# A decoder layer on one core: convolutions, low parts and norms given to other steps and engines

## The chip, the core and the metric

The kernel runs on one core of a Trainium2 chip. The metric is the device time of one execution in microseconds. TensorE (PE) multiplies, VectorE (DVE), ScalarE (ACT) and GpSimd (POOL) work elementwise, SyncE (SP) issues the transfers. Every engine takes its own instructions in order; they wait for each other by semaphores.

## The reference

One step of a hybrid decoder layer for 1024 prompt tokens and 32 sample tokens (8 sequences of 4), width 1024: adaLN, an mLSTM and a sliding-window attention branch, then a feed-forward part with a convolution over tokens. The change touches the last part alone (weights and gates left out where they don't matter):

```python
h2 = ln0(x) * (1 + scale2) + shift2
u = h2 @ w_up + b_up                       # 2 * 2816 columns
u = conv_w[2]*u[t] + conv_w[1]*u[t-1] + conv_w[0]*u[t-2] + conv_b   # causal, per column
act = gelu(u[:, :2816]) * u[:, 2816:]
x = LN2(alpha * x + gate2 * (act @ w_down + b_down))
```

The outputs also hold the last two tokens of `u` of every sequence.

## The kernel before

**Products.** All products are made of three fp32r products: each operand is a high part (`hi`, a cast by ACT) and a low part (`lo`, the rest, one subtraction). The weights come through a stream of blocks: `Stream.load` issues the transfer of a raw block into a slot of SBUF, `Stream.prep` has ACT cast the high part (L429) and `low_by` subtract the low part (L433), and frees the raw slot. `low_by` is DVE until the down groups, POOL from there on (L2120).

**Columns.** The 1056 tokens stand in the free dimension, 384 + 384 + 288 (`TT`). The 44 blocks of 128 columns of `u` are numbered 0 to 43; column `j` of the gelu half belongs to column `22 + j`. Columns 0 to 3 and 22 to 25 are made early by ordinary products; columns 20, 42, 21 and 43 by the four *direct blocks* (`up_direct`, 1607 to 1658 us), whose banks ACT empties (L1754); the other 32 by 16 *pairs* `j` = 4 to 19 (`fast`, 1270 to 1606 us), each 14 products long for both columns `j` and `22 + j`, over a ring of eight PSUM banks. When a pair's column is finished, `ff_finisher` decides: `u` of column `j` goes to DRAM as it is, column `22 + j` gets its convolution (`post`) beside the following pair and then goes to DRAM as `y`.

**Convolution.** `conv` is a generator: ACT makes the first tap and small copies (L1764 to L1769), DVE the two long taps (L1771, L1773) and two small ones for the sample tokens (L1775, L1776), with a `yield` after each part.

**Side work.** PE's instructions are the program's backbone. Each `pulse` of a product advances a program clock by its length times `rate[0]` (0.5 in the pairs, 0.9 in the direct blocks, 0.8 in the down groups); as the clock goes on, generators in `sides` are advanced by one step, and things put off by `later(us, ...)` are emitted. So the yields decide where an instruction stands in its engine's order.

**Feed.** `feed` (L1837) runs beside the direct blocks and the down groups. Item by item, in the order 4 to 11, 0, 20, 12, 13, 1, 21, 14, 15, 16, 2, 3, 17, 18, 19, it loads the two columns from DRAM, convolves column `j` (both columns for 0 to 3, 20 and 21), applies gelu (ACT, L1867), multiplies (DVE, L1872), casts the high part (ACT, L1881) and subtracts the low one (`alo`, DVE, L1886). Item n's convolution and item n-1's gelu and product share steps.

**Down groups.** `act @ w_down` runs in five groups of 5, 5, 4, 4 and 4 items (`KG`). Groups 0 to 2 go over eight output blocks `j`, each with three products (one for each part of `TT`) into the three banks `L`. Group 0 (1658 to 1717 us) writes `facc` by ACT (L1990); groups 1 to 3 add to it by DVE (L1992). Group 3 goes by tokens and is scaled by the gate; 72 transposes (`pre`) turn `facc` to rows. In group 4 (1889 to 1942 us) rows are made by products of 512 columns, two for each of nine row tiles.

**Tail.** For each row tile `i`, `add` sums on DVE, `stats` takes mean and variance (`mv`, DVE), 1/std on POOL (`rstd`, two operations) and, for `i` < 8, the factor `nbias` (POOL) and the normalisation on ACT; `gains(i - 1)` multiplies by the gain (L2179) on POOL for tiles 0 to 6 and on DVE for tile 7, and adds the bias on POOL (L2180). Tile 8, of 32 rows, goes on DVE alone (L2184, L2185).

Of the kernel before, what the change touches and what calls it, by code (L numbers as in the profile page):

```python
# [105 lines left out]
def hybrid_step(ctx: ExitStack, tc: tile.TileContext, I, O):  # L106
# [282 lines left out]
    class Stream:  # L389
        def __init__(self, specs):  # L390
            self.specs = specs
            self.raws, self.parts, self.loaded, self.limit = {}, {}, 0, len(specs)
            self.low_by = V
# [19 lines left out]
        def prep(self, i, later_lo=False):  # L413
# [24 lines left out]
            low()  # L438
# [1398 lines left out]
    def feed():  # L1837
# [3 lines left out]
        def load(n):  # L1841
            if n < len(js) and n not in got:
                ds = [uD[js[n]], yD[22 + js[n]] if 22 + js[n] in yD else uD[22 + js[n]]]
                got[n] = [slot(name="ld") for _ in ds]
                for t, d in zip(got[n], ds):
                    S.dma_start(t, d)
# [5 lines left out]
        for n in range(len(js) + 1):  # L1852
            cur = None
            if n < len(js):
                while len(free_slots) < ROOM:
                    yield
                load(n + 1)
                j, (u, y2) = js[n], got.pop(n)
                if 22 + j not in yD:
                    u2, y2 = y2, slot(name="y")  # L1860
                    yield from conv(22 + j, u2, y2)
                    drop(u2)
                    yield
                cur = slot(name="y"), y2
                taps = conv(j, u, cur[0])
            if prev:
                A.activation(prev[0], prev[0], AF.Gelu_apprx_tanh)  # L1867
            if cur:
                next(taps)
# [4 lines left out]
            if cur:  # L1874
                next(taps)
                if len(free_slots) > ROOM:
                    load(n + 2)
# [4 lines left out]
            if cur:  # L1882
                next(taps)
# [5 lines left out]
            if cur:  # L1889
                next(taps, None)  # L1890
                drop(u)
            yield
# [147 lines left out]

    def ff_finisher(j):
        return lambda blk_, z: sides.append(post(22 + j, z)) if blk_ else to_dram(uD, j, z)
# [77 lines left out]
    win.low_by = G  # L2120
# [21 lines left out]
    BY_POOL = (0, 1, 2, 3, 4, 5, 6)  # L2142
# [23 lines left out]
    def stats(i):  # L2166
        n = rows_of(i)
        mv = ln_stats(xs_[i], n)
        if i < 8:
            factor[i] = norm_factor(mv, n)  # L2170
            norm_act(xs_[i], factor[i], n)
        else:
            factor[i] = (mv, rstd(mv[:n, 1:2], n))

    def gains(i):
        n = rows_of(i)
        x = xs_[i][:n, :D]
        if i < 8:
            (G if i in BY_POOL else V).tensor_tensor(x, x, ln2g[:n, :D], op=OP.mult)  # L2179
            G.tensor_tensor(x, x, ln2b[:n, :D], op=OP.add)  # L2180
            dst = dap(O["yp"], i * 128 * D, [[D, 128], [1, D]])
        else:
# [3 lines left out]
            dst = dap(O["ys"], 0, [[D, 32], [1, D]])  # L2186
# [50 lines left out]
```

## Time and profile before

| | |
|---|---|
| median of 3 runs | 1960.11 us (1959.96 to 1962.17) |
| the profiled execution | 1961.27 us, span 1959.5 us |
| PE busy | 1904.9 us, 97% of the span |
| DVE busy | 1075.2 us, 55% |
| ACT busy | 804.9 us, 41% |
| POOL busy | 478.5 us, 24% |

The time is the span and what lies around it, 1.8 us here. The profile tells of one execution. Its times are from the span's start; the stages above are given in them.

### The profile page before, as it was taken

The numbers are of one execution on the slowest core, as the hardware profiler recorded it, in microseconds if no ns is written. First come the engines' busy times: TensorE is split into PE (matmuls) and PEld (weight loads), VectorE is DVE, ScalarE is ACT, GpSimd is POOL, SyncE is SP. The second block draws the span as 40 slices with busy tenths as digits, with TensorE's granted clock in tenths as the row PEclk, the third lists the DMA queues.
The fourth block names the chain that finished last, engine by engine and source line by source line (L and its number), as shares of the span: only waits on it lengthen the run. The fifth ranks groups of instructions, "written<-read, shape, count | busy, mean of one in ns | idle before, by whom it ended". The sixth has DMA issues, their size and how long they took to land. (4 is left out here: it accounts for less than half of the span.)

```text
span 1959.5 us, 32996 instructions
## 1 busy us (share of the span) xinstructions
PE 1904.9 (97%) x12981; PEld 1815.8 (93%) x12981; DVE 1075.2 (55%) x2293; ACT 804.9 (41%) x1796; POOL 478.5 (24%) x595
## 2 busy tenths in 40 slices
PE   6999999999999999999999999999999999999996
PEld 4899999999989989899999999999999999999884
DVE  5454444444545445332354445756666666778767
ACT  4534343343555455430322255332332336754521
POOL 2004233232022131200000243133434320222228
PEclk9999999999999999999999999999999999999998
DMA  9151524234211312298523242423232256444342
GB/s 292 48 141 19 148 25 131 59 97 79 92 67 33 113 45 86 74 338 278 165 96 101 72 127 69 143 87 123 88 120 100 96 169 214 156 132 146 128 154 89
DMA packets 233766, 232.24 MB, mean 119 GB/s; under 512 B 11665, under 2 KB 206913, under 8 KB 233577
## 3 DMA queue, kind: packets, MB, share of 16 engines
q1 hardware_dynamic: 232829, 229.51, 38.2%
q8 instruction: 102, 1.67, 0.4%
q10 hardware_dynamic: 780, 0.61, 0.1%
q14 instruction: 55, 0.45, 0.1%
HBM read 172.18 MB, written 59.93 MB: 118 GB/s over the span
## 5 line engine op out<-in xcount | busy, mean ns | idle before, releaser
L455 PE MATMUL L<-hhi,whi 128*128 128x384 f32 (+1 forms) x1600 | 526.3, 329 | 0.1
L455 PE MATMUL L<-hlo,whi 128*128 128x384 f32 (+1 forms) x1600 | 517.1, 323 | 0.0
L455 PE MATMUL L<-hhi,wlo 128*128 128x384 f32 (+1 forms) x1600 | 516.8, 323 | 0.0
L455 PEld LDWEIGHTS L<-hhi,whi 128*128 128x128 f32 x1600 | 301.6, 188 | 6.6 <-issue 4.8
L455 PEld LDWEIGHTS L<-hlo,whi 128*128 128x128 f32 x1600 | 301.8, 189 | 0.3
L455 PEld LDWEIGHTS L<-hhi,wlo 128*128 128x128 f32 x1600 | 301.4, 188 | 0.0
L433 DVE TENSOR_TENSOR wlo<-wraw,whi 128x1024 fp32r<-128x1024 f32 (+1 forms) x89 | 108.5, 1219 | 115.5 <-ACT whi L429 109.8
L455 PE MATMUL L<-mhi,whi 128*128 128x384 f32 (+1 forms) x480 | 158.6, 330 | 6.2 <-ACT whi L429 2.2
L455 PE MATMUL L<-mhi,wlo 128*128 128x384 f32 (+1 forms) x480 | 156.7, 326 | 0.9 <-DVE wlo L433 0.9
L455 PE MATMUL L<-mlo,whi 128*128 128x384 f32 (+1 forms) x480 | 156.4, 326 | 0.1
L455 PE MATMUL L<-ahi,whi 128*128 128x384 f32 (+1 forms) x432 | 141.4, 327 | 8.9 <-DVE facc L1992 7.2
L455 PE MATMUL L<-ahi,wlo 128*128 128x384 f32 (+1 forms) x432 | 139.6, 323 | 0.4 <-POOL wlo L433 0.4
L455 PE MATMUL L<-alo,whi 128*128 128x384 f32 (+1 forms) x432 | 139.5, 323 | 0.0
L429 ACT CAST whi<-wraw 128x1024 fp32r<-128x1024 f32 (+1 forms) x116 | 115.8, 998 | 18.6 <-DMA wraw<-in_w_up 8.0
L433 POOL TENSOR_TENSOR wlo<-wraw,whi 128x640 fp32r<-128x640 f32 (+1 forms) x27 | 57.7, 2138 | 239.9 <-ACT whi L429 183.3
L300 POOL TENSOR_SCALAR rstd<-mv 128x1 f32<-128x1 f32 (+1 forms) x36 | 18.2, 506 | 372.2 <-DVE mv L309 371.0
L1481 POOL TENSOR_TENSOR fw<-fraw,fw 128x512 fp32r<-128x512 f32 x32 | 42.6, 1342 | 239.3 <-ACT fw L1477 239.3
L455 PEld LDWEIGHTS L<-mhi,whi 128*128 128x128 f32 x480 | 91.4, 190 | 7.4 <-ACT whi L429 4.2
L455 PEld LDWEIGHTS L<-mhi,wlo 128*128 128x128 f32 x480 | 91.1, 190 | 1.5 <-DVE wlo L433 1.5
L455 PEld LDWEIGHTS L<-ahi,whi 128*128 128x128 f32 x432 | 81.2, 188 | 11.6 <-DVE facc L1992 4.9
L455 PEld LDWEIGHTS L<-mlo,whi 128*128 128x128 f32 x480 | 91.2, 190 | 0.4 <-DVE mlo L1672 0.3
L455 PEld LDWEIGHTS L<-ahi,wlo 128*128 128x128 f32 x432 | 81.1, 188 | 0.7 <-POOL wlo L433 0.7
(550 smaller groups left out, 4179.5 us busy)
## 6 DMA issues: line engine op xcount, KB each, us to landing
wraw<-in_w_in SPq DMA_DIRECT2D x52, 512.0 KB
ld<-ff SPq DMA_DIRECT2D x44, 528.0 KB
wada<-in_w_ada SPq DMA_DIRECT2D x44, 512.0 KB
fraw<-in_w_up SPq DMA_DIRECT2D x32, 512.0 KB
ff<-fdst SPq DMA_DIRECT2D x16, 528.0 KB
ff<-y SPq DMA_DIRECT2D x16, 528.0 KB
ff<-u SPq DMA_DIRECT2D x12, 528.0 KB
wraw<-in_w_up SPq DMA_DIRECT2D x12, 512.0 KB
```

Of the source, the lines that this page charges most:

```text
L300: G.tensor_scalar(r[:n], var, eps, None, op0=OP.add)
L429: A.copy(hi[:, :n], t[:, :n])
L433: self.low_by.tensor_tensor(lo[:, :n], t[:, :n], hi[:, :n].bitcast(F32), op=OP.subtract)
L455: T.matmul(ps[:, :nt], x[:, c], y[:, t0:t0 + nt], start=i == 0, stop=i == last)
L1481: (G if p in (1, 4) else V).tensor_tensor(lo, self.src[p], hi.bitcast(F32), op=OP.subtract)
```

## The change

It has four parts.

1. For the first six pairs (`BOTH`, columns 4 to 9) column `j` too gets its convolution beside the pairs and is stored as `y`. The feed loads both columns as they are and has no convolution for these items.
2. The steps of a feed item are cut anew: of DVE's long operations (product, two taps, `alo`) each has a step of its own, where product and second long part stood together; the item still has five yields. The next item's load moves by a step.
3. In the down groups the low parts of weights stay on DVE, and are emitted 1.6 us of the program clock after the cast (`lag`).
4. In the tail the gain of tile 3 goes from POOL to DVE, and tile 7 is treated as tile 8: normalised and scaled on DVE by two operations, with no `nbias`, ACT normalisation or POOL addition.

```diff
@@ class Stream
-            self.low_by = V
+            self.low_by, self.lag = V, 0.0
@@ Stream.prep
-            low()
+            if self.lag:
+                later(self.lag, low)
+            else:
+                low()
@@ feed
-                ds = [uD[js[n]], yD[22 + js[n]] if 22 + js[n] in yD else uD[22 + js[n]]]
+                ds = [yD[c] if c in yD else uD[c] for c in (js[n], 22 + js[n])]
...
-                cur = slot(name="y"), y2
-                taps = conv(j, u, cur[0])
+                if j in yD:
+                    cur, taps, u = (u, y2), iter(()), None
+                else:
+                    cur = slot(name="y"), y2
+                    taps = conv(j, u, cur[0])
             if prev:
                 A.activation(prev[0], prev[0], AF.Gelu_apprx_tanh)
             if cur:
-                next(taps)
+                next(taps, None)
             yield
             if prev:
                 V.tensor_tensor(prev[0], prev[0], prev[1], op=OP.mult)
                 drop(prev[1])
-            if cur:
-                next(taps)
-                if len(free_slots) > ROOM:
-                    load(n + 2)
             yield
             if prev:
                 hi, lo = slot(F32R, "ahi"), slot(F32R, "alo")
                 A.copy(hi, prev[0])
             if cur:
-                next(taps)
+                next(taps, None)
+                if len(free_slots) > ROOM:
+                    load(n + 2)
+            yield
+            if cur:
+                next(taps, None)
             yield
             if prev:
                 V.tensor_tensor(lo, prev[0], hi.bitcast(F32), op=OP.subtract)
                 drop(prev[0])
                 acts2.append((hi, lo))
             if cur:
                 next(taps, None)
-                drop(u)
-            yield
+                if u:
+                    drop(u)
             yield
@@ ff_finisher
+    BOTH = range(ND, ND + 6)
...
-        return lambda blk_, z: sides.append(post(22 + j, z)) if blk_ else to_dram(uD, j, z)
+        def done(blk_, z):
+            if blk_ or j in BOTH:
+                sides.append(post(j + 22 * blk_, z))
+            else:
+                to_dram(uD, j, z)
+        return done
@@ down groups and tail
-    win.low_by = G
+    win.lag = 1.6
-    BY_POOL = (0, 1, 2, 3, 4, 5, 6)
+    BY_POOL = (0, 1, 2, 4, 5, 6)
+    ALONE = (7, 8)
@@ stats, gains
-        if i < 8:
+        if i not in ALONE:
```

The order of DVE's instructions in the direct blocks, before (L1872 the product, L1771 and L1773 the long taps, L1886 `alo`, L1775 and L1776 the small taps, L433 the low part of weights):

```order
1880 L1872 TENSOR_TENSOR y_16354<-y_16354,ld_16245 128x1056
1881 L1771 SCALAR_TENSOR_TENSOR y_16416<-ld_16305,vT,y_16416 128x1023
1882 L1773 SCALAR_TENSOR_TENSOR y_16416<-ld_16305,vT,y_16416 128x1022
1883 L1886 TENSOR_TENSOR alo_16459<-y_16354,ahi_16458 128x1056
1884 L1775 SCALAR_TENSOR_TENSOR y_16416<-us,vT,y_16416 128x32
1885 L1776 SCALAR_TENSOR_TENSOR y_16416<-us,vT,y_16416 128x32
1886 L1872 TENSOR_TENSOR y_16416<-y_16416,ld_16306 128x1056
1887 L1771 SCALAR_TENSOR_TENSOR y_16489<-ld_16371,vT,y_16489 128x1023
1888 L1773 SCALAR_TENSOR_TENSOR y_16489<-ld_16371,vT,y_16489 128x1022
```

And after the change, at the end of the same blocks (the product is now L1878, `alo` L1893):

```order
1892 L1878 TENSOR_TENSOR ld_16316<-ld_16316,ld_16317 128x1056
1893 L1893 TENSOR_TENSOR alo_16485<-ld_16316,ahi_16484 128x1056
1894 L1878 TENSOR_TENSOR ld_16373<-ld_16373,ld_16374 128x1056
1895 L1893 TENSOR_TENSOR alo_16531<-ld_16373,ahi_16530 128x1056
1896 L433 TENSOR_TENSOR wlo_16570<-wraw_16465,whi_16569 128x640
```

The taps of these items are gone; what is left are product, `alo` and low parts.

DVE's order in down group 2, before (L1992 the addition into `facc`); POOL has the low parts there:

```order
1994 L1992 TENSOR_TENSOR facc_17165<-L_73,facc_17165 128x384
1995 L1992 TENSOR_TENSOR facc_17165<-L_71,facc_17165 128x384
1996 L1992 TENSOR_TENSOR facc_17165<-L_72,facc_17165 128x288
1997 L1992 TENSOR_TENSOR facc_17246<-L_73,facc_17246 128x384
1998 L1992 TENSOR_TENSOR facc_17246<-L_71,facc_17246 128x384
1999 L1992 TENSOR_TENSOR facc_17246<-L_72,facc_17246 128x288
2000 L1992 TENSOR_TENSOR facc_16676<-L_73,facc_16676 128x384
2001 L1872 TENSOR_TENSOR y_17731<-y_17731,ld_17599 128x1056
2002 L1771 SCALAR_TENSOR_TENSOR y_17908<-ld_17727,vT,y_17908 128x1023
2003 L1773 SCALAR_TENSOR_TENSOR y_17908<-ld_17727,vT,y_17908 128x1022
```

After the change (the addition is L1999, the taps L1774 and L1776, the small ones L1778 and L1779):

```order
2008 L433 TENSOR_TENSOR wlo_17773<-wraw_17695,whi_17772 128x640
2009 L1999 TENSOR_TENSOR facc_17157<-L_73,facc_17157 128x384
2010 L1999 TENSOR_TENSOR facc_17157<-L_71,facc_17157 128x384
2011 L1999 TENSOR_TENSOR facc_17157<-L_72,facc_17157 128x288
2012 L433 TENSOR_TENSOR wlo_17833<-wraw_17775,whi_17832 128x1024
2013 L1999 TENSOR_TENSOR facc_17241<-L_73,facc_17241 128x384
2014 L1999 TENSOR_TENSOR facc_17241<-L_71,facc_17241 128x384
2015 L1999 TENSOR_TENSOR facc_17241<-L_72,facc_17241 128x288
2016 L433 TENSOR_TENSOR wlo_17890<-wraw_17835,whi_17889 128x1024
2017 L1999 TENSOR_TENSOR facc_16675<-L_73,facc_16675 128x384
2018 L1878 TENSOR_TENSOR y_17724<-y_17724,ld_17645 128x1056
2019 L1774 SCALAR_TENSOR_TENSOR y_17910<-ld_17720,vT,y_17910 128x1023
2020 L1999 TENSOR_TENSOR facc_16675<-L_71,facc_16675 128x384
2021 L1776 SCALAR_TENSOR_TENSOR y_17910<-ld_17720,vT,y_17910 128x1022
```

A low part of 128x1024 stands between the additions of two blocks, and an addition between product with first tap and second tap.

POOL's order at the end, before (L300 and L301 `rstd`, L1600 `nbias`, L2179 the gain, L2180 the bias; `x1r` is a row tile):

```order
571 L2179 TENSOR_TENSOR x1r_18770<-x1r_18770,brow_18891 128x1024
572 L2180 TENSOR_TENSOR x1r_18770<-x1r_18770,brow_18893 128x1024
573 L300 TENSOR_SCALAR rstd<-mv 128x1
574 L301 TENSOR_TENSOR rstd<-rstd,half 128x1
575 L1600 TENSOR_SCALAR nbias<-mv,rstd 128x1
576 L2179 TENSOR_TENSOR x1r_18816<-x1r_18816,brow_18891 128x1024
577 L2180 TENSOR_TENSOR x1r_18816<-x1r_18816,brow_18893 128x1024
578 L300 TENSOR_SCALAR rstd<-mv 32x1
579 L301 TENSOR_TENSOR rstd<-rstd,half 32x1
580 L2180 TENSOR_TENSOR x1r_18898<-x1r_18898,brow_18893 128x1024
```

After the change (the gain is L2196, the bias L2197):

```order
543 L2196 TENSOR_TENSOR x1r_18769<-x1r_18769,brow_18891 128x1024
544 L2197 TENSOR_TENSOR x1r_18769<-x1r_18769,brow_18893 128x1024
545 L300 TENSOR_SCALAR rstd<-mv 128x1
546 L301 TENSOR_TENSOR rstd<-rstd,half 128x1
547 L2196 TENSOR_TENSOR x1r_18815<-x1r_18815,brow_18891 128x1024
548 L2197 TENSOR_TENSOR x1r_18815<-x1r_18815,brow_18893 128x1024
549 L300 TENSOR_SCALAR rstd<-mv 32x1
550 L301 TENSOR_TENSOR rstd<-rstd,half 32x1
```

Tile 7's `nbias` and its addition are gone from POOL. DVE's last rows after the change, where L2200 and L2201 are the two operations on DVE alone (the same two rows stood there for tile 8 only, behind one L2179 for tile 7):

```order
2210 L309 BN_AGGR mv<-st 32x2
2211 L2200 SCALAR_TENSOR_TENSOR x1r_18898<-x1r_18898,mv,brow_18891 128x1024
2212 L2201 SCALAR_TENSOR_TENSOR x1r_18898<-x1r_18898,rstd,brow_18893 128x1024
2213 L2200 SCALAR_TENSOR_TENSOR x1r_18930<-x1r_18930,mv,brow_18891 32x1024
2214 L2201 SCALAR_TENSOR_TENSOR x1r_18930<-x1r_18930,rstd,brow_18893 32x1024
```

## Rows read from the trace of the kernel before

**Rows 1.** The page, busy time and share of the span of each engine, with the number of instructions.

```profile
PE 1904.9 (97%) x12981; PEld 1815.8 (93%) x12981; DVE 1075.2 (55%) x2293; ACT 804.9 (41%) x1796; POOL 478.5 (24%) x595
```

**Rows 2.** Five stretches of the core: from and to in us, length, busy us of each engine with its instructions, then the granted clock of TensorE as a share of 2.4 GHz, the DMA share and GB/s. The first lies in the pairs, the second in down group 1, the last is the end of the kernel.

```profile
1300.00:1350.00 50.00, 50.00 (x414) 50.00 (x413) 32.43 (x59) 15.89 (x38) 17.54 (x14) 1.00 0.38 129
1700.00:1750.00 50.00, 49.90 (x317) 49.51 (x316) 32.58 (x42) 29.40 (x63) 10.59 (x7) 1.00 0.36 115
1750.00:1800.00 50.00, 46.74 (x287) 45.89 (x287) 41.32 (x51) 24.31 (x46) 12.88 (x6) 1.00 0.46 153
1800.00:1850.00 50.00, 46.37 (x278) 45.74 (x276) 44.05 (x55) 26.81 (x50) 13.17 (x5) 1.00 0.36 118
1900.00:1960.00 60.00, 42.24 (x187) 32.04 (x185) 44.26 (x65) 9.96 (x8) 46.43 (x41) 0.89 0.18 73
```

**Rows 3.** The timeline of PE: start and length in us, engine, line, operation, output<-inputs and shape, and in brackets the idle time before it with what ended it. The nine rows stand apart in time.

```profile
1607.44 0.41 PE L455 MATMUL L<-mhi,whi 128*128 128x384 f32 x1 [1.65 <-DVE fdst L1530]
...
1648.64 0.44 PE L455 MATMUL L<-mhi,whi 128*128 128x384 f32 x1 [2.00 <-ACT u L1754]
...
1658.42 0.44 PE L455 MATMUL L<-ahi,whi 128*128 128x384 f32 x1 [0.59 <-ACT u L1754]
...
1672.26 0.40 PE L455 MATMUL L<-ahi,whi 128*128 128x288 f32 x1 [0.99 <-ACT facc L1990]
...
1774.12 0.41 PE L455 MATMUL L<-ahi,whi 128*128 128x384 f32 x1 [1.96 <-DVE facc L1992]
...
1792.57 0.40 PE L455 MATMUL L<-ahi,whi 128*128 128x288 f32 x1 [0.96 <-DVE facc L1992]
...
1825.58 0.44 PE L455 MATMUL L<-ahi,whi 128*128 128x384 f32 x1 [2.05 <-DVE facc L1992]
...
1841.68 0.42 PE L455 MATMUL L<-ahi,whi 128*128 128x384 f32 x1 [1.58 <-DVE facc L1992]
...
1882.42 0.66 PE L198 MATMUL PD<-cst,facc 128*128 128x128 f32 x4 [1.46 <-DVE x1r L1950]
```

**Rows 4.** Two stretches of 2 us behind the wait of 2.00 us, columns as in group 2.

```profile
1650.00:1652.00 2.00, 2.00 (x8) 2.00 (x7) 0.66 (x3) 1.21 (x2) 0.00 (x0) 0.53 0.34 85
1652.00:1654.00 2.00, 2.00 (x9) 2.00 (x9) 0.00 (x0) 2.00 (x7) 0.00 (x0) 0.62 1.01 382
```

**Rows 5.** The timelines of POOL and of DVE around 1770 us, and one DVE row from the direct blocks, in which POOL is idle; columns as in group 3.

```profile
1767.87 1.97 POOL L433 TENSOR_TENSOR wlo<-wraw,whi 128x640 fp32r<-128x640 f32 x1 [6.35 <-DMA wraw<-in_w_down]
1771.09 4.84 POOL L433 TENSOR_TENSOR wlo<-wraw,whi 128x1024 fp32r<-128x1024 f32 x2 [1.25 <-DVE alo L1886]
...
1768.69 2.26 DVE L1886 TENSOR_TENSOR alo<-y,ahi 128x1056 fp32r<-128x1056 f32 x1
1770.87 0.24 DVE L1775 SCALAR_TENSOR_TENSOR y<-us,vT,y 128x32 f32<-128x32 f32 x1
1771.15 2.35 DVE L1776 SCALAR_TENSOR_TENSOR y<-us,vT,y 128x32 f32<-128x32 f32 x1
1773.43 1.37 DVE L1992 TENSOR_TENSOR facc<-L,facc 128x384 f32<-128x384 f32 x3
...
1642.39 1.25 DVE L1886 TENSOR_TENSOR alo<-y,ahi 128x1056 fp32r<-128x1056 f32 x1
```

**Rows 6.** DVE's instructions from 1606 to 1890 us grouped by line, operation and shape: line, engine, operation, output<-inputs, shape and count, then busy us and mean ns of one, then the idle time before them.

```profile
L1771 DVE SCALAR_TENSOR_TENSOR y<-ld,vT,y 128x1023 f32<-128x1023 f32 x28 | 35.8, 1278 | 3.6 <-ACT y L1764 3.6
L1886 DVE TENSOR_TENSOR alo<-y,ahi 128x1056 fp32r<-128x1056 f32 x22 | 35.7, 1623 | 2.3 <-ACT ahi L1881 2.3
L1776 DVE SCALAR_TENSOR_TENSOR y<-us,vT,y 128x32 f32<-128x32 f32 x29 | 12.7, 438 | 1.0
L433 DVE TENSOR_TENSOR wlo<-wraw,whi 128x1024 fp32r<-128x1024 f32 x3 | 3.7, 1226 | 5.2 <-ACT whi L429 5.2
L433 DVE TENSOR_TENSOR wlo<-wraw,whi 128x640 fp32r<-128x640 f32 x1 | 0.8, 824 | 4.1 <-DMA ld<-ff 4.1
```

**Rows 7.** A stretch of 21 us in the pairs (columns as in group 2) and, from the table of waits of 1290 to 1606 us, a row with engine, tile and line, what it waited for, us in total, times, longest us.

```profile
1311.00:1332.00 21.00, 21.00 (x176) 21.00 (x175) 13.19 (x25) 6.38 (x15) 8.33 (x7) 1.00 0.30 102
...
DVE y L1771 <- ACT y L1764: 18.4, 16, 1.9
```

**Rows 8.** Two rows of the table of waits of 1595 to 1900 us, columns as in group 7.

```profile
ACT y L1867 <- DVE y L1776: 41.6, 16, 4.2
DVE wlo L433 <- ACT whi L429: 5.2, 2, 4.4
```

**Rows 9.** The timeline of POOL at the end, the multiplications of tiles 5 and 6; columns as in group 3.

```profile
1939.28 2.40 POOL L2179 TENSOR_TENSOR x1r<-x1r,brow 128x1024 f32<-128x1024 f32 x1
...
1945.40 2.35 POOL L2179 TENSOR_TENSOR x1r<-x1r,brow 128x1024 f32<-128x1024 f32 x1
```

**Rows 10.** The timeline of DVE at the end: the variance of tile 8, the multiplication of tile 7, the last operation; columns as in group 3.

```profile
1944.97 0.20 DVE L309 BATCH_NORM_AGGREGATE mv<-st 32x2 f32<-32x12 f32 x1
...
1946.75 2.08 DVE L2179 TENSOR_TENSOR x1r<-x1r,brow 128x1024 f32<-128x1024 f32 x1 [1.58 <-ACT x1r L1604]
...
1952.85 3.35 DVE L2185 SCALAR_TENSOR_TENSOR x1r<-x1r,rstd,brow 32x1024 f32<-32x1024 f32 x1 [0.75 <-POOL rstd L301]
```

More of the change, by code (lines that the diff above doesn't have):

```diff
@@ L2177, in gains @@
         x = xs_[i][:n, :D]
-        if i < 8:
+        dst = dap(O["yp"], i * 128 * D, [[D, 128], [1, D]]) if i < 8 else dap(O["ys"], 0, [[D, 32], [1, D]])
+        if i not in ALONE:
             (G if i in BY_POOL else V).tensor_tensor(x, x, ln2g[:n, :D], op=OP.mult)
             G.tensor_tensor(x, x, ln2b[:n, :D], op=OP.add)
-            dst = dap(O["yp"], i * 128 * D, [[D, 128], [1, D]])
         else:
@@ L2185, in gains @@
             V.scalar_tensor_tensor(x, x, r[:n], ln2b[:n, :D], op0=OP.mult, op1=OP.add)
-            dst = dap(O["ys"], 0, [[D, 32], [1, D]])
         S.dma_start(dst, x)
```

## The prediction

> **What bounds the kernel now.** The busy shares come first: TensorE (PE) is busy 97% of the span, VectorE (DVE) 55% [rows 1]. What can be won is PE's idle time where the change touches, plus what follows the last product; so I read stretches next. In a stretch of the pairs PE is busy for all of its 50 us [rows 2]: nothing is to be had there, and something can be lost. From 1750 to 1850 PE falls short by 3.3 and 3.6 us of 50, while DVE is busy for 41.3 and 44.1; in the last 60 us PE is idle for 17.8, nearly all of it after the last product. PE's timeline names the waits [rows 3]: 1.65 us for the last pair's sum, 2.00 and 0.59 for banks that ScalarE (ACT) empties in the direct blocks (L1754), 0.99 for ACT's evacuation in down group 0 (L1990), 1.96, 0.96, 2.05 and 1.58 for DVE's additions into `facc` (L1992), 1.46 for DVE in the transposes. That is 13.2 us, 0.7% of the time. The 2.00 us wait has a tail: the granted clock of the four microseconds behind it is 0.53 and 0.62 of 2.4 GHz [rows 4], about the lower level. At those shares 4 us did the work of 2.3, so up to 1.7 us went to the clock; I take 1.5.
>
> **Why DVE is late in the down groups.** Look at 1767 to 1775 [rows 5]. While POOL (GpSimd) computes low parts (L433), DVE's operations with two inputs stretch: `alo` takes 2.26 us where the same form takes 1.25 with POOL idle, and the 32-element L1776 takes 2.35 where its twin L1775 just ahead takes 0.24. `alo` starts while the 128x640 operation of POOL runs and ends 1.1 us after that has ended (1769.84); L1776 ends with the first of POOL's two 128x1024 operations (1771.09 + 2.42 = 1773.5). So the one waits for the other. Three additions follow, and PE's wait of 1.96 us ends on the first. From 1606 to 1890, L1886 has a mean of 1623 ns and L1776 of 438 [rows 6]; above 1.25 and 0.25 that is 22 x 0.37 + 29 x 0.19 = 13.7 us of such stretching, in these two forms alone.
>
> **The change, part by part.**
>
> *Six more convolutions beside the pairs.* DVE is busy 13.2 us and ACT 6.4 in 21 us there [rows 7], the length of one pair (336 us for 16). An added convolution costs DVE two taps of 1.28 us [rows 6], two small ones of 0.25 and, like the present one, a wait for ACT of 18.4 / 16 = 1.15 us [rows 7]: 4.2 us, so DVE goes to about 17.4 of 21. ACT at most doubles, to 12.8. The store per column stays one, at another place of the program. The price I put on this is nothing; what covers it is DVE's 3.6 us left in each pair and a ring of eight banks, each one product long. With that cover gone it costs the shortfall: were the 4.2 us to take 9 (every operation stretched as in [rows 5]), that is 1.2 us in each of six pairs, some 7 us. The feed loses six convolutions of 3.06 us on DVE, 18.4 us, in the direct blocks and the start of group 0, where ACT waits for DVE.
>
> *The direct blocks.* ACT's gelu waits for DVE's last tap 16 times, 41.6 us in all [rows 8], and ACT's emptying of the banks stands behind it in ACT's order: hence PE's 2.00 and 0.59. With no taps in the first six items, DVE's order there holds only the product, `alo` and weights' low parts, and gelu finds its input in place. So 2.00 + 0.59 + 1.5 of clock = **4.1 us** go, between 2.6 (one small wait turns up elsewhere) and 4.3.
>
> *One long operation a step.* For later items the mult and the first tap, 1.26 + 1.28 us, no longer stand in one step, so an addition has at most one long operation of a step ahead of it. But gelu now follows directly on the step with the last taps, so ACT's wait for it stays for them. In group 0, where ACT evacuates, the first items with taps come at its end: I take **1.0 us**, the 0.99, between 0 and 1.4.
>
> *Low parts on DVE.* POOL loses 27 operations, DVE gains 12 of 1.23 and 15 of 0.82 us, 27.1 us [rows 6], and loses at least 13.7 us of stretching and the 18.4 of the convolutions: its total does not grow, where they stand matters. PE's matmuls take 49.90 / 317 = 0.157 us in an undisturbed stretch [rows 2]; a block of three products is 36 of them at four tiles, 5.7 us, and 45 at five, 7.1. In that time DVE has three additions (1.37 us [rows 5]), the larger part of an item (1.25 + 1.28 + 1.28 + 1.25 + 0.5 = 5.6 us) and a low part in one of two blocks (1.23): 7.5 us against 5.7 in groups 2 and 3 while items last. So DVE stays the later engine there, now by sums and not by exclusion, and the three `L` banks cover two products. I regain somewhat over half of the four waits with 1.96, 0.96, 2.05 and 1.58, in all 6.6: **4.0 us**, between 0 (the load only moves) and 6.6. The lag of 1.6 us puts the low part behind ACT's cast; where the cast itself waits for a transfer, DVE now waits as POOL did, with additions queued behind it. DVE met two such waits in the direct blocks, 5.2 us [rows 8].
>
> One rule speaks against this part. The Trainium skill's page "Perfetto Trace Analysis", section "Optimizing Scalar/DVE Operations", says that a saturated DVE may be relieved by giving work even to GpSimd, though the two share a port, so that it might not help. By the first half, taking 27 operations back onto a DVE busy for 41 to 44 of 50 us would lose the 4.0 us, which is R1 below. By the second half POOL's work was never free, and the trace agrees with that half, at 2.26 us for 1.25.
>
> *Transposes.* DVE has there a low part in place of a stretched addition: 1.46 us stays, and so does the 1.65 at 1607.
>
> *Tail.* POOL multiplies and adds a tile in 2.4 us each with small operations between, 6.12 us from one tile's mult to the next [rows 9], and is never idle; the last tiles' norms queue behind it. DVE's mult of tile 7 waits 1.58 us for ACT (which needs POOL's nbias), and DVE's last operation waits 0.75 us for POOL's rstd [rows 10]. Without tile 3's mult (2.4 us), POOL's mult of tile 6 starts near 1943.0 instead of 1945.4, its add ends near 1947.8, and both rstd are there by 1948.8. DVE has the variance of tile 8 at 1945.2, then four operations of 1.28 us; two of them meet POOL, and I add what the 2.08 and a 3.35 us row show above 1.28, 2.9 us, and 0.4 for gaps: 1953.6 instead of 1956.2. **2.6 us** (1.5 to 4).
>
> Sum: 4.1 + 1.0 + 4.0 + 2.6 = 11.7. The profiled execution took 1961.27 us (span 1959.5 and 1.8 around it), the median 1960.11. 1961.27 - 11.7 = 1949.6; set against the median it is 1948.4. I say **1949.0**.
>
> **Rivals.**
> R1, *the low parts only move load*: the `facc` waits and group 0's keep their size. For it: DVE at 41 and 44 of 50 [rows 2]. Against it: 13.7 us of stretching goes. Gain 4.1 + 2.6 = 6.7: about 1954. Chance 0.20.
> R2, *all waits go*: 4.1 + 1.4 + 6.6, the transposes' 1.46 and 4 in the tail, 17.6 us: 1943. For it: the longest waits end behind a stretched operation [rows 3, 5]. Against it: the 7.5 us for 5.7. Chance 0.12.
> R3, *slower*: low parts stand in DVE's order, waiting for ACT's cast and the weights' transfer, additions queued behind. With 27 of them, the gain is gone when each costs PE 11.7 / 27 = 0.43 us, and it is slower by 0.2% from 0.58 us on. At 0.7 it is 1949 + 19 = 1968. Against it: in the direct blocks DVE's two waits of that kind ended in no wait of PE on DVE [rows 3]; POOL's waits for casts say little, since POOL had nothing else to do. Chance 0.07.
> R4, *the pairs lose PE time*: DVE needs more than 21 us a pair, 1.2 us over in each of six, 7 us: 1956.7. Against it: 17.4 by the rows, and POOL there is busy 8.3 of 21. Chance 0.07; it is also the time if the edits hardly change anything.
> The forecast has 0.54.
>
> 0.2% is 3.9 us, about what a measurement of this kernel tells from no change. The range for 8 in 10 is **1943.5 to 1956.5**: the terms' lower ends give 2.6 + 0 + 0 + 1.5 = 4.1 us, 1956, the upper 4.3 + 1.4 + 6.6 + 4 = 16.3, 1944; R1 and most of R2 lie in it. Faster: the forecast, R2, and four fifths of R1, 0.82. Same: the rest of R1 and R4, 0.11. Slower: R3, 0.07.
>
> **What would show it.** Right: from 1610 to 1660 no PE wait on L1754 and no clock near 0.5; no POOL row at L433 in the down groups; `alo` at 1.25 us and the small taps at 0.25 throughout; waits on L1992 shorter by half, and behind runs of long DVE operations; DVE busy about 17 of 21 us in the first six pairs with PE at 100%; the last DVE operation 11.6 us after the last product instead of 14.2. Wrong: DVE rows at L433 waiting several us for ACT's cast and PE waits on L1992 that end behind them; PE idle in the first six pairs; four stretched DVE operations in the tail.

## The result and the profile after

The changed kernel takes 1947.87 us in the median (1944.14 to 1949.63, 4 runs) against 1961.14 (1959.96 to 1964.21, 4 runs): a ratio of 0.9928, interval 0.9916 to 0.994, 13.3 us less. Forecast were 1949.0 us and a range of 1943.5 to 1956.5. The profiled execution of after is the fastest of its four (1944.14 us, span 1942.4).

The busy shares, as in [rows 1], and five stretches with the columns of [rows 2] (the first two in the pairs and in down group 1, the fourth holds the start of group 3, the last is the end):

```profile
PE 1899.3 (98%) x12981; PEld 1813.5 (93%) x12981; DVE 1082.9 (56%) x2322; ACT 803.6 (41%) x1795; POOL 424.1 (22%) x565
```

```profile
1300.00:1350.00 50.00, 50.00 (x414) 50.00 (x412) 42.47 (x67) 20.06 (x52) 25.57 (x17) 1.00 0.30 100
1700.00:1750.00 50.00, 50.00 (x313) 49.98 (x311) 39.64 (x56) 29.01 (x59) 0.00 (x0) 1.00 0.45 148
1750.00:1800.00 50.00, 50.00 (x314) 50.00 (x314) 42.07 (x62) 22.61 (x48) 0.00 (x0) 1.00 0.41 140
1800.00:1850.00 50.00, 44.87 (x257) 43.84 (x257) 34.45 (x48) 24.97 (x44) 0.00 (x0) 0.93 0.39 119
1890.00:1942.00 52.00, 38.66 (x168) 29.11 (x166) 41.74 (x60) 8.72 (x7) 42.52 (x36) 0.90 0.21 84
```

PE is now busy without a gap from 1700 to 1800, where it fell short by 3.3 us in 1750 to 1800 before, with DVE still busy for 42.1 of 50 us. POOL has nothing to do in these stretches of the down groups. One stretch got worse: 44.87 of 50 in 1800 to 1850, at a clock of 0.93.

PE's timeline names the waits that are left, with the columns of [rows 3]:

```profile
1602.26 0.41 PE L458 MATMUL L<-mhi,whi 128*128 128x384 f32 x1 [0.68 <-DVE fdst L1533]
...
1822.50 0.69 PE L458 MATMUL L<-ahi,wlo 128*128 128x384 f32 x1 [4.83 <-DVE wlo L433]
1822.99 0.52 PE L458 MATMUL L<-ahi,whi 128*128 128x384 f32 x1
1823.31 0.52 PE L458 MATMUL L<-alo,whi 128*128 128x384 f32 x1
...
1828.73 0.34 PE L458 MATMUL L<-ahi,whi 128*128 128x384 f32 x1
1828.90 0.34 PE L458 MATMUL L<-alo,whi 128*128 128x384 f32 x1
...
1833.88 0.41 PE L458 MATMUL L<-ahi,whi 128*128 128x384 f32 x1 [0.26 <-DVE facc L1999]
...
1863.90 1.26 PE L198 MATMUL PD<-cst,facc 128*128 128x128 f32 x8 [0.60 <-DVE x1r L1957]
...
1868.86 1.25 PE L198 MATMUL PD<-cst,facc 128*128 128x128 f32 x8 [0.53 <-DVE x1r L1957]
```

Of the eight waits behind ACT and DVE that [rows 3] shows ahead of the transposes, from 1607 on, 0.68 us at the last pair and 0.26 us of one addition are left, and there is a new one: 4.83 us for a low part (L433) at the third matmul of group 3's second weight block. Behind it the next matmuls of 384 columns start 0.32 us apart, where from 1828.73 on they start 0.17 apart; in 1822 to 1828 the granted clock is 0.50, the lower level of 1.2 GHz. Some eighteen matmuls ran so, from 1822.99 to 1828.73; at 0.174 us each instead of 0.319 they would have taken 2.6 us less. The section on the experiments shows that this did not make the stage longer.

Where the time went, by stages: PE's first matmul of the direct blocks, of group 0 and of group 4, then the end of tile 8's last addition and of DVE's last operation (all read from the timelines):

| | before | after | gain |
|---|---|---|---|
| start of the direct blocks | 1607.44 | 1602.26 | 5.2, of it 4.2 ahead of the pairs |
| direct blocks | 50.98 | 46.41 | 4.6 |
| down groups 0 to 3 | 231.04 | 227.22 | 3.8 |
| group 4, to the last addition | 54.22 | 54.21 | 0.0 |
| from there to DVE's last operation | 12.52 | 9.41 | 3.1 |

The 4.2 us stand in a part of the program that the change doesn't touch (the last section says what they are); they are not the change's. Without them the table's stages add up to 12.5 us; the medians differ by 13.3.

### The profile page after: what moved, and what is told of

It reads as the page before. It is cut to its first block, busy times and chain, and to the rows that moved or that the text cites. A ratio compares the mean times of both kernels' runs of the same rounds, so it can differ in the third digit from the quotient of the medians.

```text
span 1942.4 us, 32942 instructions
## 1 busy us (share of the span) xinstructions
PE 1899.3 (98%) x12981; PEld 1813.5 (93%) x12981; DVE 1082.9 (56%) x2322; ACT 803.6 (41%) x1795; POOL 424.1 (22%) x565
## 5 line engine op out<-in xcount | busy, mean ns | idle before, releaser
L433 DVE TENSOR_TENSOR wlo<-wraw,whi 128x1024 fp32r<-128x1024 f32 (+1 forms) x116 | 135.4, 1168 | 123.1 <-ACT whi L429 122.6
L300 POOL TENSOR_SCALAR rstd<-mv 128x1 f32<-128x1 f32 (+1 forms) x36 | 19.1, 530 | 658.0 <-DVE mv L309 657.0
L1484 POOL TENSOR_TENSOR fw<-fraw,fw 128x512 fp32r<-128x512 f32 x32 | 46.9, 1477 | 232.0 <-ACT fw L1480 232.0
L458 PEld LDWEIGHTS L<-alo,whi 128*128 128x128 f32 x432 | 82.1, 190 | 0.0
```

Source lines behind the costliest of these rows:

```text
L300: G.tensor_scalar(r[:n], var, eps, None, op0=OP.add)
L433: self.low_by.tensor_tensor(lo[:, :n], t[:, :n], hi[:, :n].bitcast(F32), op=OP.subtract)
L458: T.matmul(ps[:, :nt], x[:, c], y[:, t0:t0 + nt], start=i == 0, stop=i == last)
L1484: (G if p in (1, 4) else V).tensor_tensor(lo, self.src[p], hi.bitcast(F32), op=OP.subtract)
```

## The experiments

All are the changed kernel with an edit unless they say otherwise. Each was timed against the kernel before. The stage times are read as in the table above; it has a column for each at the end of this section.

**Each part undone.** The first part, with one line:

```diff
-    BOTH = range(ND, ND + 6)
+    BOTH = ()
```

> The changed kernel with the first part undone: columns 4 to 9 are convolved in the feed again (BOTH is empty). Theory: the direct blocks lose what they won, PE waits on ACT's L1757 return (2 to 3 us with one slow clock behind them), the stage from the first direct block to group 0 goes from 46.4 back to 49 to 51 us; ratio to the kernel before about 0.9955 instead of 0.993. Rival: the stretch of work there was made short by the steps cut anew (second part) and the stage stays at 46.4 to 47, ratio 0.993. Pairs: PE at 100% in both.

Measured: 0.9984 (0.9975 to 0.9992), 1958.31 us. The stage is 52.2 us and PE's waits on ACT's emptying are back, with one more in group 0 (timeline of PE):

```profile
1649.35 0.44 PE L458 MATMUL L<-mhi,whi 128*128 128x384 f32 x1 [2.56 <-ACT u L1757]
...
1654.90 0.40 PE L458 MATMUL L<-mhi,whi 128*128 128x288 f32 x1 [1.06 <-ACT u L1757]
...
1659.18 0.44 PE L458 MATMUL L<-ahi,whi 128*128 128x384 f32 x1 [0.84 <-ACT u L1757]
...
1666.16 0.69 PE L458 MATMUL L<-ahi,whi 128*128 128x384 f32 x1 [4.09 <-ACT u L1757]
```

The theory holds for the place and is too small for the price: the last wait of 4.09 us stands in group 0, which needs a bank that ACT empties behind the same queue, and from 1665 to 1672 the granted clock is 0.53, about the lower level. Down groups 0 to 3 take 230.9 us instead of 227.2. Undone, the part costs 10 us.

The second part undone:

```diff
             if cur:
+                next(taps, None)
+                if len(free_slots) > ROOM:
+                    load(n + 2)
             yield
             if prev:
                 hi, lo = slot(F32R, "ahi"), slot(F32R, "alo")
...
-            if cur:
-                next(taps, None)
-                if len(free_slots) > ROOM:
-                    load(n + 2)
-            yield
...
+            yield
             yield
```

> The changed kernel with the feed's old steps (second part undone: product and first tap in one step again, the empty step at the item's end). Theory: the steps decide only how long an addition waits on DVE; the waits on L1999 come back in part, some 1 to 3 us in groups 0 to 3; ratio 0.994 to 0.995. Rival: the steps are worth nothing once POOL is out of the way, ratio 0.993.

Measured: 0.9931 (0.992 to 0.9943), 1948.26 us: the rival. The down groups take 228.1 us instead of 227.2, with four waits around the start of group 3 (1.08, 3.64, 0.88, 1.12) in place of two. That is at most 1 us, which the timing can't tell from nothing.

The third part undone (`win.low_by = G` in place of `win.lag = 1.6`):

> The changed kernel with the third part undone: POOL computes the low parts in the down groups, at once. Theory of exclusion: DVE's alo and small taps are stretched again (mean of alo above 1.5 us), additions are late, several us of PE waits on L1999 come back in groups 1 to 3, while the one wait of 4.8 us for a low part at the start of group 3 goes; the down groups then take 227 to 231 us, ratio 0.993 to 0.995. Rival R1 (the low parts only move load): the down groups are as long or shorter, 224 to 227 us, ratio 0.9915 to 0.993.

Measured: 0.996 (0.9948 to 0.9972), 1953.84 us; down groups 231.9 us. The theory holds (`alo`'s mean over the later sixteen is 1.47 us, 1.25 in after), and the price is beyond its upper end. PE waits on additions again and the wait for the low part of group 3 falls to 0.63 us (PE's timeline):

```profile
1766.37 0.42 PE L458 MATMUL L<-ahi,whi 128*128 128x384 f32 x1 [1.94 <-DVE facc L1999]
...
1816.71 0.45 PE L458 MATMUL L<-ahi,whi 128*128 128x384 f32 x1 [1.01 <-DVE facc L1999]
...
1827.97 0.44 PE L458 MATMUL L<-ahi,wlo 128*128 128x384 f32 x1 [0.63 <-POOL wlo L433]
...
1832.73 0.45 PE L458 MATMUL L<-ahi,whi 128*128 128x384 f32 x1 [2.74 <-DVE facc L1999]
```

The fourth part undone:

```diff
-    BY_POOL = (0, 1, 2, 4, 5, 6)
-    ALONE = (7, 8)
+    BY_POOL = (0, 1, 2, 3, 4, 5, 6)
+    ALONE = (8,)
```

> The changed kernel with the old tail (fourth part undone: POOL has tile 3's gain and tile 7 goes through ACT and POOL). Theory: from the last addition of tile 8 to DVE's last operation 12.5 us instead of 9.4, ratio 0.9945. Rival: POOL's backlog came from its low parts before and is gone, so the tail stays below 11 us; ratio 0.9935.

Measured: 0.9938 (0.9926 to 0.995), 1949.77 us. From the last addition to DVE's last operation it is 12.1 us, against 9.4 in after: the theory by the profile (2.7 us), while the times, 1.9 us above those of after, can't tell the two apart.

**Parts alone.** The kernel before with the first part only (the hunks of `feed`'s load and `cur` and of `ff_finisher`):

> The kernel before with the first part alone: six more convolutions beside the pairs. If the four terms add up: the direct blocks 46.4 us instead of 51.0, about 1 us less at the last pair, the down groups as before (231) with their waits on L1992: ratio 0.997. Rival, from the 10 us that undoing this part cost in e1_no_six: it is worth twice as much also alone, since group 0 begins with fewer items behind, down groups 228 or less: ratio 0.995.

Measured: 0.9972 (0.9963 to 0.9981), 1954.57 us; direct blocks 46.4, the wait at the last pair 0.68, down groups 232.2. As the sum has it; the rival falls.

The kernel before with the third part only (`lag` and the hunk of `prep`):

> The kernel before with the third part alone: low parts on DVE with the lag of 1.6 us. If the terms add up: waits on L1992 mostly gone, down groups 227 us instead of 231, direct blocks 51 as before: ratio 0.998. Rival: with all taps still in the feed DVE is too full in group 0 to 2, the lows only move load, and waits grow where ACT and DVE are behind at the start of group 0: down groups 231 us or more, ratio 1.0 or above.

Measured: 0.9952 (0.9938 to 0.9965), 1950.97 us. Direct blocks 50.8, down groups **223.9**: 7.1 us less than before, more than the 3.8 of the whole change. The rival that lows only move load falls, and so does the theory's number. Now DVE's `alo` and smalls have their plain durations (grouped rows, columns as in [rows 6]). Three addition waits are left, 1.07 us at 1819.6, 0.95 at 1835.0 and 0.89 at 1838.3. PE's missing 3.3 us of 1750 to 1800 [rows 2] are gone, of the 3.6 of 1800 to 1850 still 3.1 are there:

```profile
L1889 DVE TENSOR_TENSOR alo<-y,ahi 128x1056 fp32r<-128x1056 f32 x22 | 27.5, 1251 | 1.7 <-ACT ahi L1884 1.7
L1779 DVE SCALAR_TENSOR_TENSOR y<-us,vT,y 128x32 f32<-128x32 f32 x29 | 7.3, 252 | 1.0
```

```profile
1750.00:1800.00 50.00, 50.00 (x311) 50.00 (x310) 42.99 (x62) 26.92 (x53) 0.00 (x0) 1.00 0.48 155
1800.00:1850.00 50.00, 46.90 (x281) 45.66 (x280) 43.23 (x60) 25.27 (x46) 0.00 (x0) 1.00 0.34 115
```

So parts one and three alone give 5.5 and 9.4 us by their ratios, with the tail's 2.7 some 17.6, the whole change 13 to 14. Taken together, the intervals of these ratios are about as wide as the difference, but the stages show a loss too: the down groups take 223.9 us with the third part alone and 227.2 in the whole change. The 4.83 us wait is the place. Neither e12_low_alone nor e1_no_six has a PE wait on a low part in group 3, e2_old_steps has one of 3.64 us: it takes the first and the third part together.

**Exclusion or place.** POOL gets the same work a second time, and DVE's order stays as it is:

```diff
                 self.low_by.tensor_tensor(lo[:, :n], t[:, :n], hi[:, :n].bitcast(F32), op=OP.subtract)
+                if self.lag:
+                    G.tensor_tensor(t[:, :n], t[:, :n], hi[:, :n].bitcast(F32), op=OP.subtract)
                 drop(t)
```

> The changed kernel with POOL doing a subtraction of the same size in place on the raw weights right behind each of DVE's low parts in the down groups; its result is used by nothing. DVE's order is the same. Theory of exclusion: DVE's operations with two SBUF inputs are stretched again (alo's mean above 1.45 us instead of 1.25), PE waits on L1999 of 3 to 6 us come back, down groups 230 to 234 us, ratio 0.9945 to 0.997. Rival (POOL cost time before only because its low parts came late for PE): alo stays at 1.25 to 1.3, down groups 227 to 228.5 us, ratio 0.993.

Measured: 1.0026 (1.0014 to 1.0037), 1966.32 us, slower than before; down groups 242.5 us. `alo`'s mean is 1.41 us over the later sixteen, just short of the 1.45 expected, and a timeline shows the mechanism as [rows 5] did (POOL first, then DVE; line numbers are higher by two in this kernel):

```profile
1819.84 3.36 POOL L435 TENSOR_TENSOR wraw<-wraw,whi 128x1024 f32<-128x1024 f32 x1 [11.76 <-DVE wlo L433]
...
1838.78 6.55 POOL L435 TENSOR_TENSOR wraw<-wraw,whi 128x1024 f32<-128x1024 f32 x2 [15.58 <-DMA wraw<-in_w_down]
```

```profile
1821.33 2.98 DVE L1895 TENSOR_TENSOR alo<-y,ahi 128x1056 fp32r<-128x1056 f32 x1
...
1840.16 2.94 DVE L1776 SCALAR_TENSOR_TENSOR y<-ld,vT,y 128x1023 f32<-128x1023 f32 x1
1843.14 3.27 DVE L1778 SCALAR_TENSOR_TENSOR y<-ld,vT,y 128x1022 f32<-128x1022 f32 x1
```

```profile
L1895 DVE TENSOR_TENSOR alo<-y,ahi 128x1056 fp32r<-128x1056 f32 x16 | 22.6, 1413 | 1.2 <-issue 1.2
```

Two taps of 1.28 us take 2.94 and 3.27 while POOL's two operations run (1838.78 to 1845.33). The theory of exclusion holds for these operations. Its price was set too low (242.5 against 230 to 234): the raw slot is also held for POOL's work, so the 15 us need not all be exclusion. The run does not part the two.

**The new wait.** In the trace of after, the 4.83 us end a chain over four engines (SP's timeline, then ACT's, then DVE's):

```profile
1813.97 5.55 SPq L408 DMA_DIRECT2D wraw<-in_w_down  x12
```

```profile
1812.51 1.04 ACT L429 CAST whi<-wraw 128x1024 fp32r<-128x1024 f32 x1
1817.99 1.04 ACT L429 CAST whi<-wraw 128x1024 fp32r<-128x1024 f32 x1 [4.43 <-DMA wraw<-in_w_down]
1818.94 1.08 ACT L1873 ACTIVATE y<-y 128x1056 f32<-128x1056 f32 x1
```

```profile
1820.05 1.26 DVE L1878 TENSOR_TENSOR y<-y,ld 128x1056 f32<-128x1056 f32 x1 [3.69 <-ACT y L1873]
1821.23 2.35 DVE L433 TENSOR_TENSOR wlo<-wraw,whi 128x1024 fp32r<-128x1024 f32 x2
```

SP issues three raw blocks from 1813.97 on, group 3's third block the first of them. Before it SP waits 11.1 us for a DVE operation, the second tap (L1776) that ends at 1813.9 (that the block takes the slot of this tap's input is read from the order). ACT's cast of that block waits 4.43 us for the transfer. The gelu behind it in ACT's order ends at 1820.0, DVE's product waits 3.69 us for it, and both low parts stand behind the product, though the first one's cast (1812.51) had long been done. PE needs that one at 1817.7. Five runs take links out.

Lag 0 everywhere (`win.lag = 0.0`):

> The changed kernel with lag 0: the low part is emitted right after the cast. Theory (the 4.8 us wait of PE for a low part at the start of group 3 comes from a chain: weights' transfer late, ACT's cast waits for it, gelu behind the cast, DVE's product behind gelu, the low parts behind the product): both low parts stand ahead of the product now, the second waits for the late cast itself, and the first addition of group 3 comes near 22 us after 1800: PE waits some 2 to 3 us on L1999 instead of 4.8 on L433; elsewhere a few waits for casts. Ratio 0.992 to 0.994. Rival (the low part's own place is the cause): the wait goes altogether, ratio 0.989 to 0.990.

Measured: 0.9931 (0.9918 to 0.9943); PE waits 2.26 us on L1999 there, and 1.28, 1.93 and 1.11 around it; down groups 227.7. As expected.

Lag 0 for the first of the two alone:

```diff
     def down_by_tokens(gi):
         a = operands(gi)
+        lag, win.lag = win.lag, 0.0
         win.prep(dn_at[gi] + 1)
+        win.lag = lag
```

> The changed kernel with lag 0 for one low part alone, the first at the start of group 3 (it then stands ahead of DVE's product that waits for gelu). By the chain above PE no longer waits on L433 but on L1999 about 3.6 us later in the same block, since the additions are still behind that product: the down groups 225 to 227 us, ratio 0.992. Rival: the wait goes altogether, down groups 220 us, ratio 0.989 to 0.990.

Measured: 0.9922 (0.991 to 0.9935); the wait is 3.72 us, and on an addition, as the chain has it (3.6); down groups 226.5 (PE's timeline):

```profile
1826.44 0.52 PE L458 MATMUL L<-ahi,whi 128*128 128x384 f32 x1 [3.72 <-DVE facc L1999]
```

The transfer earlier, nothing else:

```diff
     def down_group(gi):
...
                 win.done(s_)
+            if gi == 2 and j == 6:
+                win.load(dn_at[3] + 2)
```

> The changed kernel with the raw weights of the third block of group 3 loaded earlier, at the next to last output block of group 2, and nothing else. By the chain, ACT's cast no longer waits 4.4 us for the transfer, gelu and the product come some 4 us earlier, PE's wait for the low part falls from 4.8 to about 1.3 us and the granted clock behind it stays at 1: down groups 220 to 222 us, ratio 0.9895 to 0.991. Rival (the place of the low part): the wait stays at 3.5 us or more, ratio 0.9925.

Measured: 0.9928 (0.9913 to 0.9942), down groups 225.8. The wait is 3.37 us, not 1.3, which is near the rival's 3.5. ACT's timeline says why the chain's forecast missed: both casts now stand together and wait for DVE's `alo`, not for the transfer.

```profile
1819.55 2.00 ACT L429 CAST whi<-wraw 128x1024 fp32r<-128x1024 f32 x2 [2.97 <-DVE alo L1893]
1821.45 1.08 ACT L1873 ACTIVATE y<-y 128x1056 f32<-128x1056 f32 x1
```

Slots are handed out in the order in which they came free; with one taken earlier, the cast's slot is one that `alo` reads last. That step is read from the code, the wait from the trace. So this run does not part the theory from its rival.

Both edits:

> Both: the earlier load of e7_load_early and the first low part ahead of the product as in e6_first_low. By the chain no PE wait over 0.6 us is left in the down groups but the transposes', the clock stays at 1 there: 219 to 220 us, ratio 0.989. Rival: something else at the start of group 3 is late in its turn (the slot of the earlier load, ACT), 2 us or more of waits stay.

Measured: 0.9908 (0.9893 to 0.9924), 1944.07 us, down groups 224.7 and the clock at 1. Waits of 1.56, 0.69, 0.89 and 1.08 us on additions stay: the rival, though in a better time.

Last, the first low part at lag 0 and the late cast moved out of gelu's way:

```diff
-                if k < 3:
+                if k == 0:
+                    win.load(s_ + 2)
+                elif k < 3:
                     win.prep(s_ + 2 if k < 2 else s_ + 1)
                     win.load(s_ + 3)
...
                     down_block(gi, j, ti, a)
+                    if k == 0 and j == 0:
+                        win.prep(s_ + 2)
+                        win.load(s_ + 3)
```

> The changed kernel with lag 0 for the first low part of group 3 (as e6_first_low), and the cast of the third weight block of group 3 moved behind the first product of that group (its transfer is still issued at the same place), so that ACT's gelu no longer stands behind a cast that waits for the transfer. By the chain the product and the additions of group 3 come 3 to 4 us earlier, no PE wait above 1.2 us is left there and the clock stays at 1: down groups 220 to 223 us, ratio 0.9895 to 0.991. Rival: DVE is the late engine there by its sums, the waits on L1999 come one after another and add up to 3 us or more; down groups 224 us and more, ratio 0.991 to 0.992.

Measured: 0.9908 (0.9895 to 0.9922), 1943.24 us, down groups 223.3 us, as good as with the third part alone. Between the theory and the rival: the 4.83 us wait and the low clock are gone, and three waits on additions, 1.59, 0.89 and 1.11 us, follow one another (PE's timeline):

```profile
1826.63 0.41 PE L458 MATMUL L<-ahi,whi 128*128 128x384 f32 x1 [1.59 <-DVE facc L1999]
...
1829.86 0.44 PE L458 MATMUL L<-ahi,whi 128*128 128x384 f32 x1 [0.89 <-DVE facc L1999]
...
1833.34 0.42 PE L458 MATMUL L<-ahi,whi 128*128 128x384 f32 x1 [1.11 <-DVE facc L1999]
```

This version is 17 to 18 us below the kernel before and beats the changed kernel by 3.9 us of that stage; the intervals of the two ratios (0.9895 to 0.9922, 0.9916 to 0.994) overlap at their ends.

What these runs change is the start of DVE's first addition of group 3. Here is that start, counted from group 0's start, the time from it to group 4, and the granted clock in the 10 us around it (all from the timelines and windows, us):

| kernel | first addition of group 3 | from it to group 4 | clock |
|---|---|---|---|
| after | 174.8 | 52.4 | 0.66 |
| e4, same instructions here | 174.8 | 52.4 | 0.83 |
| e5 | 174.4 | 53.3 | 0.83 |
| e6 | 174.0 | 52.5 | 0.83 |
| e7 | 173.4 | 52.4 | 0.66 |
| e8 | 172.2 | 52.4 | 1.00 |
| e9 | 169.9 | 53.4 | 1.00 |

So the low clock did not lengthen the stage: the time from that addition on is no shorter with less of it or none, and PE then waits longer for the additions behind (1.11 us in e4_old_tail in place of 0.26 in after). The chain of DVE's and ACT's operations sets the pace there, not PE, and what the stage loses is the lateness of DVE's first addition.

And all stages of all runs:

| kernel | direct blocks | groups 0 to 3 | last addition to end | ratio |
|---|---|---|---|---|
| before | 51.0 | 231.0 | 12.5 | |
| after | 46.4 | 227.2 | 9.4 | 0.9928 |
| e1, first part undone | 52.2 | 230.9 | 9.5 | 0.9984 |
| e2, second undone | 46.4 | 228.1 | 9.3 | 0.9931 |
| e3, third undone | 46.4 | 231.9 | 9.5 | 0.996 |
| e4, fourth undone | 46.4 | 227.2 | 12.1 | 0.9938 |
| e11, first alone | 46.4 | 232.2 | 12.5 | 0.9972 |
| e12, third alone | 50.8 | 223.9 | 12.0 | 0.9952 |
| e10, POOL's work twice | 46.4 | 242.5 | 9.9 | 1.0026 |
| e5, lag 0 | 46.4 | 227.7 | 9.4 | 0.9931 |
| e6, first low part at lag 0 | 46.4 | 226.5 | 9.5 | 0.9922 |
| e7, transfer earlier | 46.4 | 225.8 | 9.5 | 0.9928 |
| e8, both | 46.4 | 224.7 | 9.5 | 0.9908 |
| e9, cast later | 46.4 | 223.3 | 9.3 | 0.9908 |

## Why the prediction was right, step by step

*Six convolutions beside the pairs, price nothing.* Right in the price. PE is busy for all of 21 us in the changed pairs. DVE's load was set too low: 17.4 us, of which 1.15 were waiting and not work, where this stretch is busy for 19.5 (another pair, 1340 to 1361, for 18.2). POOL works there too, and the second tap has a mean of 1.6 us instead of 1.28: the five that overlap with POOL take 1.48 to 2.32 us, the others 1.27 or 1.28 (a stretch of after with the columns of [rows 2]; its taps of 1290 to 1400 us, grouped as in [rows 6]):

```profile
1311.00:1332.00 21.00, 21.00 (x175) 21.00 (x174) 19.53 (x33) 8.40 (x22) 9.51 (x7) 1.00 0.37 128
```

```profile
L1776 DVE SCALAR_TENSOR_TENSOR y<-fdst,vT,y 128x1022 f32<-128x1022 f32 x11 | 17.7, 1605 | 0.0
```

So the cover was 1.5 us there and not 3.6; more such pairs would have little room.

*Direct blocks, 4.1 us.* Measured 4.6, and the same with the first part alone. Every term was there: both waits on L1754 and the clock behind the first; ACT's waits for DVE's last tap fell from 16 times and 41.6 us [rows 8] to this row of the waits of 1590 to 1890:

```profile
ACT y L1873 <- DVE y L1779: 21.6, 9, 4.3
```

What I had left as it is, the 1.65 us at 1607, fell to 0.68 us in every kernel with the first part and stayed at 1.66 without it: 1 us not forecast.

*One operation a step and group 0, 1.0 us.* The waits of group 0 are gone in after, but with the old steps too, and with the first part alone (e11_six_alone has none there, with the third alone 0.35 us is left): they went with the first part, and the 1.0 us was put down to the wrong one. The second part's own worth is within the uncertainty of the measurement.

*Low parts on DVE, 4.0 us.* The size came near (3.8 us for all four groups, 5.0 forecast for them), by an argument that was half wrong, and in part by luck. I reasoned that DVE stays the later engine by its sums, 7.5 us in a block of 5.7. The step counted an item in every block; the feed's 22 items, six of them now without taps, are spread over some 230 us, one in 10.5. With POOL silent DVE kept up from 1750 to 1800: it is busy 42.1 us of 50 with PE at 50.0, and `alo` is back at its plain 1.25 us (after, grouped as in [rows 6]):

```profile
L1893 DVE TENSOR_TENSOR alo<-y,ahi 128x1056 fp32r<-128x1056 f32 x16 | 20.0, 1249 | 1.2 <-ACT ahi L1883 1.2
L433 DVE TENSOR_TENSOR wlo<-wraw,whi 128x1024 fp32r<-128x1024 f32 x15 | 18.3, 1222 | 5.6 <-ACT whi L429 5.2 <-DMA ld<-ff 0.4
L433 DVE TENSOR_TENSOR wlo<-wraw,whi 128x640 fp32r<-128x640 f32 x16 | 13.2, 823 | 12.4 <-ACT whi L429 12.3
```

At the start of group 3 it did stay the later engine, as the additions' pace in the table of the first additions shows. With the third part alone, of the four waits' 6.6 us 2.9 are left in three waits (e12_low_alone), so 3.6 were won there, "somewhat over half" as forecast; the stage as a whole won 7.1 us, of it 2.3 by smaller waits that this term left out (on additions, on a low part, in group 0 and in the transposes), and some 1.1 us that can't be read as waits. What took this 7.1 down to 3.8 was R3's mechanism, low parts that stand in DVE's order behind something that waits for ACT and a transfer, at one place and not at many: DVE's first addition of group 3 comes 3.8 us later in after (174.8 us from group 0's start) than in e12_low_alone (171.0), and earlier by 4.9 once the late cast is moved (e9_cast_later). I had it as a rival of its own with a chance of 0.07 and no term in the sum, while the order of DVE's rows at the start of group 3 (product, two low parts, addition) was there to be read beforehand. In e12_low_alone ACT's cast is as late (3.91 us of waiting, there for PE), but the low parts stand ahead of the product and PE doesn't wait for them. That the two errors, a stage gain of 7.1 us and a loss of 3.3, left the sum near the forecast is luck.

The rule of the Trainium skill, page "Perfetto Trace Analysis", section "Optimizing Scalar/DVE Operations", was weighed by its halves: the runs bear out the second, that giving DVE's work to GpSimd might not help. The same groups take 231.0 us with the low parts on GpSimd and 223.9 with them on DVE (e12_low_alone), and 242.5 when GpSimd works beside DVE again (e10_pool_twice, where the held slot may have a share).

*Transposes, nothing.* 0.60 and 0.53 us are left of 0.57 and 1.46: some 0.9 us gained that I left out.

*Tail, 2.6 us.* Measured 3.1 (2.7 by e4_old_tail). POOL's mult of tile 6 starts 0.2 us before the last addition ends, before the change 1.7 us behind it. DVE's timeline of after from the last addition on, with the four normalising operations at its end:

```profile
1929.42 0.68 DVE L2178 TENSOR_TENSOR x1r<-L,x1r 32x512 f32<-32x512 f32 x1
...
1931.52 1.80 DVE L2200 SCALAR_TENSOR_TENSOR x1r<-x1r,mv,brow 128x1024 f32<-128x1024 f32 x1
1933.42 3.18 DVE L2201 SCALAR_TENSOR_TENSOR x1r<-x1r,rstd,brow 128x1024 f32<-128x1024 f32 x1
1936.52 1.27 DVE L2200 SCALAR_TENSOR_TENSOR x1r<-x1r,mv,brow 32x1024 f32<-32x1024 f32 x1
1938.24 1.27 DVE L2201 SCALAR_TENSOR_TENSOR x1r<-x1r,rstd,brow 32x1024 f32<-32x1024 f32 x1 [0.45 <-POOL rstd L301]
```

Two are stretched, 1.80 and 3.18 us: 2.4 us above 1.28 where I had 2.9.

## What to carry to other kernels

An operation that VectorE takes back from GpSimd can cost less than it seems, because GpSimd's copy was paid for by VectorE's two-input operations: look for operations that end where GpSimd's end, and price the move by the excess. Behind such a move, look in the order for places where the moved work stands behind an operation that waits for a third engine: one such place (a late transfer, a cast, a gelu, a product, two low parts) took back nearly half of the gain in that stage. Work that is moved to where its engine has time to spare beside a busy TensorE can be free (six convolutions cost PE nothing here), and the gain lies with the engine behind it in the chain (here ScalarE's emptying of banks). The low clock behind a wait was no loss where TensorE was not the later engine (group 3 here).

## What the runs showed of the hardware that was not expected

The 4.2 us that the profiled execution of after is ahead before the pairs come from unchanged instructions. Two jumps of 1.5 us stand in the timelines, near 512 and 1172 us; the rest comes in smaller steps. At the first, the same sixteen 64x16 matmuls (1.96 us) run in both; behind them the granted clock falls in the execution of before and stays at 1 in that of after (windows of 6 us, columns as in [rows 2]):

```profile
510.00:516.00 6.00, 6.00 (x37) 5.90 (x36) 3.93 (x17) 0.77 (x3) 0.00 (x0) 0.79 0.58 178
1172.00:1178.00 6.00, 6.00 (x30) 5.96 (x29) 1.23 (x1) 2.08 (x3) 0.24 (x1) 0.72 1.16 324
```

```profile
510.00:516.00 6.00, 6.00 (x44) 5.90 (x43) 3.72 (x17) 1.84 (x8) 0.00 (x0) 1.00 0.58 178
1172.00:1178.00 6.00, 5.79 (x38) 5.48 (x37) 2.52 (x4) 5.07 (x9) 0.00 (x0) 1.00 0.73 241
```

Over the fourteen profiles of this study the clock of 500 to 530 us is 0.94 in five and 1.00 in nine, that of 1165 to 1185 is 0.83 or 0.91 in eleven and 1.00 in three. So the same instructions lose 1.5 us to the clock, or don't, from one execution to the next; kernels that differ by a few us are better compared by the length of a stage than by one span.
